# The input norm of an encoder layer, split between rows and the transposed side, with the residual rows made later

## The chip, the cores and the metric

The kernel runs on one core of one Trainium2 chip. The core has five engines that work side by side, each with its own in-order stream: PE (matrix products; its weight loads are shown apart as PEld), DVE (vector), ACT (scalar functions and copies), POOL (a general engine) and SP (which issues most transfers). They wait for one another through semaphores. What counts is the time of one execution in device microseconds, as the median of several runs. Beside it stands one profiled execution with the start and length of every instruction.

## The reference

One layer of a bidirectional encoder, 512 tokens of width 1024. What matters here is its head:

```python
h = layer_norm(x, ln_in_g, ln_in_b)            # (x - mean) * rsqrt(var + eps) * g + b
mix = parallel_mixer(h, ...)                   # h @ w_in: q, k, v of two attention families, and so on
h = layer_norm(DEEPNORM_ALPHA * h + mix, ...)  # the residual uses alpha * h again
mem_n = layer_norm(mem, ...)                   # 256 memory rows, for a later attention
```

The mixer projects h into window heads (8 query heads, 2 key/value heads, with a sink) and into three groups of 8 dilated heads. Then follow memory attention and a gated convolution, which the change doesn't touch.

## The kernel before, in words

**Data.** The rows of x lie in four blocks of 128 tokens, `h[0]` to `h[3]`, two each in the tiles `oA` and `oB`, which later take the attention outputs. Every product in full precision is made of three: operands are split in a rounded half (`hi`, a cast on ACT) and the rest (`lo`, a subtraction on DVE), and hi·hi, hi·lo and lo·hi are summed. So h is wanted transposed (feature on the partition) in two tiles, `Thi` and `Tlo`, and each weight as `hi` and `lo`.

**The prologue** (up to the line 505) makes h, its transposed halves, and the value projection of dilated group 0 on the way: 4 blocks times 24 products of 512 columns, called `hh` (hi weight, hi h), `lh` (hi weight, lo h) and `hl` (lo weight, hi h), into `g` tiles for blocks 0 and 1 and one `s` tile for blocks 2 and 3. For each block there are the statistics (`stats`, DVE; for block 3 `sums`, on ACT), the reciprocal deviation on POOL (`power`, L109), `gain` (L341, L343: subtract the mean, times g, two halves of 512) and `shift` (L348: times the deviation, plus b) on DVE, `turn` (eight 128x128 transposes on PE, L355, into the PSUM tiles `t` and `o`), `t_hi` (cast on ACT, L362) and `t_lo` (DVE, L367). g and b are spread over all partitions by products with a matrix of ones (L387, L390). `spill` (L371) writes alpha·h to memory through ACT, a block at a time, and with it the residual for later. `v_hi` and `v_lo` (L282) split the value weights. Before the first product PE is given small filler products (`busy`), as many as `WARM` says. PE, DVE and ACT all follow the written order here; the block is under a manual schedule.

**The mixer** follows from line 936 on. PE's order is still as written: projections of 24 products are cut into by *items*, pieces of attention work that wait in a queue until their inputs have been ready for some products. The item A0 is the first of the near dilated group: scores on PE, a row minimum on DVE (L725), exponentials on ACT (L728), transposes of the result on PE (L682). W0 is the first window item (L815, L819, the same lines for transposes). Each projection of a q or k ends in a rotation (`rope`): a product with the cosines on DVE (L528), a shuffle on DVE (L529), a product (L530) and a sum (L531) on POOL. DVE, ACT, POOL and SP are not ordered by hand here: a list scheduler places their instructions by its own cost estimates, and what it chose is then their fixed order. Weight loads go through SP into a ring of three buffers (`raw`). The 512 KB tiles for gains and shifts share two buffers under the tag `gb`.

Of the kernel before, what the change touches and what calls it, by code (L numbers as in the profile page):

```python
# [72 lines left out]
def hymba_layer(ctx: ExitStack, tc: tile.TileContext, A, cst_d, out):  # L73
# [173 lines left out]
    nc.gpsimd.memset(ones_t, 1.0)
# [6 lines left out]
    gin = wpool.tile([P, D], F32, tag="gb", bufs=2, name="gin")  # L254
    gt = halves(gin)
    sbt = s_tile()
    bt = [sbt[:, n, :] for n in range(2)]
# [78 lines left out]

    def gain(b):
        th = halves(h[b])
        for i in range(2):
            if ("mu", b) in LN:  # L340
                nc.vector.scalar_tensor_tensor(th[i], th[i], LN["mu", b], gt[i], ALU.subtract, ALU.mult)  # L341
            else:
                nc.vector.scalar_tensor_tensor(th[i], th[i], LN["nm", b], gt[i], ALU.add, ALU.mult)  # L343

    def shift(b):
        th = halves(h[b])
        for i in range(2):
            nc.vector.scalar_tensor_tensor(th[i], th[i], LN["rs", b], bt[i], ALU.mult, ALU.add)  # L348
# [15 lines left out]
    def t_lo(b):
        for i, src in enumerate(LN["T", b]):
            hi, lo = (t[:, 4 * i : 4 * i + 4, b * P : (b + 1) * P] for t in hT)
            nc.vector.tensor_tensor(lo, src, hi.bitcast(F32), ALU.subtract)  # L367
# [1192 lines left out]
```

## Time and profile before

| | us |
|---|---|
| median of 3 runs (lowest, highest) | 910.73 (910.62, 910.97) |
| the profiled execution | 911.27 |
| its span | 909.5 |
| PE busy in the span | 896.6 |
| DVE busy | 560.2 |
| ACT busy | 385.0 |
| first product of the value projection starts at | 13.10 |
| first product of the mixer starts at | 40.16 |

The span runs from the first to the last instruction on the engines; the execution's own time is somewhat longer. A row of a time line gives the start, the length, the engine, the line and operation, the output and the inputs with their sizes, the count of such instructions in a row and, in brackets, how long the engine was idle just before and what ended that. A row of groups gives, after the bar, the sum of busy time in us and the mean of one in ns, then the idle time before them. Names are those of the program's tiles: `Thi`, `Tlo` are the halves of h transposed, `raw`, `hi`, `lo` a weight and its halves, `zs` a tile of scratch, `mx` the memory rows.

### The profile page before, as it was taken

What the parts mean: (1) busy time and instruction counts of PE and PEld (TensorE: products, weight loads), DVE (VectorE), ACT (ScalarE), POOL (GpSimd) and SP (SyncE); (2) the same over time, 40 slices, a digit from 0 to 9 for tenths busy, and PEclk for the clock granted to TensorE, in tenths of its full rate; (3) what the DMA queues carried; (4) which work ended last, traced back from release to release, by engine and by line L of the source; (5) the groups of instructions that cost most, each with busy time, mean ns of one, the idle gap of its engine ahead of it and who ended that gap; (6) DMA issues with size and microseconds to landing.
All of it is one profiled execution on the core that took longest, in us unless ns stands there. A gap on an engine that the chain in (4) does not pass through costs nothing.

```text
span 909.5 us, 12905 instructions
## 1 busy us (share of the span) xinstructions
PE 896.6 (99%) x5097; PEld 768.3 (84%) x5097; DVE 560.2 (62%) x956; ACT 385.0 (42%) x672; POOL 127.2 (14%) x106
## 2 busy tenths in 40 slices
PE   9999999999999999999999999999999999999996
PEld 7778987898878798788988889799999999888885
DVE  7975146335446667869466576877777767433346
ACT  4563436415545576315454224344444345222210
POOL 1064033431443420010000010000000000000001
PEclk9999999999999999999999999999999999999999
DMA  6762041214221337316222304233333354223201
GB/s 220 225 213 70 24 139 47 73 67 117 70 70 47 93 117 233 138 46 171 85 70 70 93 25 129 82 93 93 95 114 94 96 160 140 93 93 103 83 23 70
DMA packets 116942, 92.84 MB, mean 102 GB/s; under 512 B 12472, under 2 KB 100752, under 8 KB 116882
## 3 DMA queue, kind: packets, MB, share of 16 engines
q1 hardware_dynamic: 116048, 89.80, 32.4%
q10 hardware_dynamic: 834, 2.22, 0.6%
q8 instruction: 40, 0.66, 0.3%
q14 instruction: 20, 0.16, 0.1%
HBM read 87.82 MB, written 4.19 MB: 101 GB/s over the span
## 4 chain that ended last, share of the span: by engine, by line
PE 95%; DVE 3%; ACT 1%; DMA 1%; issue 0%; POOL 0%; DVEq 0%; ACTq 0%
PE g L168 54%; PE s L168 24%; PE o L168 5%; PE t L168 4%; PE o L694 3%; PE s L682 2%; PE s L208 1%; DMA vt<-in_ln_in_g_dram 1%; PE s L1225 0%; DVE lo L282 0%; DVE oA L348 0%; DVE st L312 0%; DVE Tlo L367 0%; POOL zs L530 0%; DVE mx L1206 0%
## 5 line engine op out<-in xcount | busy, mean ns | idle before, releaser
L138 DVE TENSOR_TENSOR lo<-raw,hi 128x1024 fp32r<-128x1024 f32 x126 | 157.2, 1249 | 86.6 <-ACT hi L136 85.9
L136 ACT CAST hi<-raw 128x1024 fp32r<-128x1024 f32 x126 | 132.3, 1051 | 141.5 <-PE g L168 92.5
L168 PE MATMUL g<-Thi,hi 128*128 128x512 f32 x240 | 94.8, 395 | 0.0
L168 PE MATMUL g<-Tlo,hi 128*128 128x512 f32 x240 | 94.2, 393 | 0.0
L168 PE MATMUL g<-Thi,lo 128*128 128x512 f32 x240 | 94.0, 392 | 0.0
L109 POOL TENSOR_TENSOR rs<-ve,mhalf 128x1 f32<-128x1 f32 x18 | 15.3, 852 | 524.9 <-DVE ve L115 513.6
L530 POOL TENSOR_TENSOR zs<-zs,rsn 128x512 f32<-128x512 f32 x29 | 59.2, 2040 | 147.5 <-DVE zs L529 147.5
L168 PE MATMUL g<-Uhi,hi 128*128 128x512 f32 (+1 forms) x224 | 77.5, 346 | 1.0 <-ACT hi L136 1.0
L168 PE MATMUL g<-Ulo,hi 128*128 128x512 f32 (+1 forms) x224 | 77.1, 344 | 0.0
L168 PE MATMUL g<-Uhi,lo 128*128 128x512 f32 (+1 forms) x224 | 77.0, 344 | 0.0
L168 PE MATMUL g<-hi,Thi 128*128 128x512 f32 x184 | 71.6, 399 | 0.0
L168 PE MATMUL g<-hi,Tlo 128*128 128x512 f32 x184 | 70.9, 395 | 0.5 <-DVE Tlo L1173 0.5
L168 PE MATMUL g<-lo,Thi 128*128 128x512 f32 x184 | 70.7, 395 | 0.4 <-DVE lo L282 0.4
L528 DVE TENSOR_TENSOR zs<-g,rc 128x512 f32<-128x512 f32 x29 | 20.0, 689 | 68.2 <-PE g L168 31.6
L168 PE MATMUL g<-x,hi 128*128 128x256 f32 x320 | 58.8, 284 | 0.0
L168 PEld LDWEIGHTS g<-Thi,hi 128*128 128x128 f32 x240 | 45.1, 188 | 11.1 <-issue 0.9
L168 PEld LDWEIGHTS g<-Tlo,hi 128*128 128x128 f32 x240 | 45.1, 188 | 10.3 <-issue 1.4
L168 PEld LDWEIGHTS g<-Thi,lo 128*128 128x128 f32 x240 | 45.1, 188 | 9.3
L168 PEld LDWEIGHTS g<-x,hi 128*128 128x128 f32 x320 | 50.0, 192 | 0.5 <-issue 0.3
L168 PEld LDWEIGHTS g<-hi,Tlo 128*128 128x128 f32 x184 | 42.2, 230 | 6.4 <-DVE Tlo L1173 1.0
L168 PEld LDWEIGHTS g<-Uhi,hi 128*128 128x128 f32 x224 | 42.5, 190 | 5.8 <-ACT hi L136 1.2
L138 DVE TENSOR_TENSOR lo<-act,hi 128x512 fp32r<-128x512 f32 x22 | 14.8, 690 | 52.8 <-ACT hi L136 52.8
(363 smaller groups left out, 2091.8 us busy)
## 6 DMA issues: line engine op xcount, KB each, us to landing
raw<-in_w_in_dram SPq DMA_DIRECT2D x37, 512.0 KB, 3.8
raw<-in_w_gate_dram SPq DMA_DIRECT2D x22, 512.0 KB, 3.8
raw<-in_w_up_dram SPq DMA_DIRECT2D x22, 512.0 KB, 3.9
raw<-in_w_down_dram SPq DMA_DIRECT2D x22, 512.0 KB, 3.4
raw<-in_w_xk_dram SPq DMA_DIRECT2D x8, 512.0 KB, 3.9
raw<-in_w_xv_dram SPq DMA_DIRECT2D x8, 512.0 KB, 3.5
raw<-in_w_xq_dram SPq DMA_DIRECT2D x8, 512.0 KB, 4.6
raw<-in_w_xo_dram SPq DMA_DIRECT2D x8, 512.0 KB, 3.5
```

What stands on the lines that cost most here:

```text
L109: nc.gpsimd.tensor_tensor(out_, in_, mhalf, ALU.pow)
L136: nc.scalar.copy(hi, raw)
L138: (eng or nc.vector).tensor_tensor(lo, raw, hi.bitcast(F32), ALU.subtract)
L168: on_pe(nc.tensor.matmul(o, l, r, start=first, stop=last))
L208: on_pe(nc.tensor.transpose(ps[:, i // 4, f : f + P], t[:, i * P : (i + 1) * P], ident))
L528: nc.vector.tensor_tensor(zc, ps, rc, ALU.mult)
L530: nc.gpsimd.tensor_tensor(sh, sh, rsn, ALU.mult)
L682: nc.tensor.transpose(tp[:, k, :], s_, ident)
L694: nc.tensor.matmul(o[HJ[j], t0:t1], lhs(j), rhs(j), start=i == 0, stop=i == len(parts) - 1)
```

## The change

**The norm in two places.** `norm(b)` (L314) makes (x − mean)·deviation on the rows, one DVE instruction over 1024 columns in place of four over 512. Gain and shift are put on after the transpose, where a feature is a partition and g and b are one number each per partition: `t_gain` (L334 on ACT, L336 on DVE) reads the transposed PSUM tile in pieces of 128x128, since each piece has its own columns of g and b, four pieces for each half, and writes into `vt`. Then `t_hi` casts from there (L340) and `t_lo` subtracts from there (L344). ACT makes the pieces for the first half of blocks 0 and 1 and for all of blocks 2 and 3, DVE the second half of blocks 0 and 1. g and b arrive as 16 rows of 128 by two small transfers and are turned by one PE transpose into `gcol`, 128x16. The broadcast products, the two zeroings of `vt` and ACT's two copies of g are gone. All four blocks now take their statistics on DVE.

**The residual rows in the mixer.** `spill(b)` no longer copies on ACT. Since the rows in `oA` and `oB` lack g and b, four DVE instructions of 128x512 for each block (L349) make alpha·rows·g and then add alpha·b, in place, with two broadcast tiles loaded again through SP (`gb`, 512 KB each); then one transfer on ACT's queue (L350). Blocks 0 and 1 stand after the item A0 in the program, 2 and 3 after the window projection; where they come in DVE's order is up to the list scheduler, but the four of a block keep their order. The memory norm's tiles (`gm`) share the buffers of `gb`, so their loads wait for the last spill.

**Order.** The written order of the prologue is new, as is the number of fillers. In the lists below a row is a line of the program, the operation, the output and the inputs; x2 means two of them in a row.

DVE, prologue, from the split of the value weights and block 2 on (`st`, `mv`, `ve` belong to the statistics, `sm` and `nm` to the sums on ACT). Before:

```order
L282 TENSOR_TENSOR lo<-raw,hi 128x1024
L329 TENSOR_SCALAR nm<-sm 128x1
L282 TENSOR_TENSOR lo<-raw,hi 128x1024
L341 SCALAR_TENSOR_TENSOR oB<-oB,mv,gin 128x512 x2
L348 SCALAR_TENSOR_TENSOR oB<-oB,rs,s 128x512 x2
L282 TENSOR_TENSOR lo<-raw,hi 128x1024
L343 SCALAR_TENSOR_TENSOR oB<-oB,nm,gin 128x512 x2
L333 TENSOR_SCALAR ve<-sm 128x1
L367 TENSOR_TENSOR Tlo<-t,Thi 128x4x128
L367 TENSOR_TENSOR Tlo<-o,Thi 128x4x128
L282 TENSOR_TENSOR lo<-raw,hi 128x512 x2
```

and now, from the statistics of block 2 on:

```order
L309 BN_STATS st<-oB 128x6 x2
L113 BN_AGGR mv<-st 128x2
L115 TENSOR_SCALAR ve<-mv 128x1
L314 TENSOR_SCALAR oB<-oB,mv,rs 128x1024
L277 TENSOR_TENSOR lo<-raw,hi 128x1024
L344 TENSOR_TENSOR Tlo<-vt,Thi 128x4x128 x2
L309 BN_STATS st<-oB 128x6 x2
L113 BN_AGGR mv<-st 128x2
L115 TENSOR_SCALAR ve<-mv 128x1
L277 TENSOR_TENSOR lo<-raw,hi 128x512 x2
L314 TENSOR_SCALAR oB<-oB,mv,rs 128x1024
```

The last piece of the value weights (`lo` in two halves of 512) stood and stands behind `Tlo` of block 2; new between the two are the statistics of block 3.

PE, prologue, from the transposes of block 2 on. Before:

```order
L355 MATMUL t<-cst,oB 128x128 x4
L355 MATMUL o<-cst,oB 128x128 x4
L168 MATMUL g<-lo,Thi 128x512 x4
L168 MATMUL s<-hi,Thi 128x512 x8
L168 MATMUL s<-hi,Tlo 128x512 x8
L168 MATMUL s<-lo,Thi 128x512 x6
```

and now:

```order
L321 MATMUL t<-cst,oB 128x128 x4
L321 MATMUL o<-cst,oB 128x128 x4
L168 MATMUL g<-hi,Tlo 128x512 x8
L168 MATMUL g<-lo,Thi 128x512 x12
L321 MATMUL t<-cst,oB 128x128 x4
L321 MATMUL o<-cst,oB 128x128 x4
L168 MATMUL s<-hi,Thi 128x512 x8
```

All twelve remaining `hl` products of blocks 0 and 1 (`g<-lo,Thi`) now come before the products of block 2; the last eight of them use the last two pieces of the value weights.

DVE in the mixer, around the item A0 (the row minima, `ISA`). Before:

```order
L528 TENSOR_TENSOR zs<-g,rc 128x512
L529 STREAM_SHUFFLE zs<-g 128x512
L138 TENSOR_TENSOR lo<-raw,hi 128x1024
L528 TENSOR_TENSOR zs<-g,rc 128x512
L529 STREAM_SHUFFLE zs<-g 128x512
L138 TENSOR_TENSOR lo<-raw,hi 128x1024
L725 ISA pu,stT<-s,cst 128x128
```

and now:

```order
L349 SCALAR_TENSOR_TENSOR oA<-oA,gb 128x512
L138 TENSOR_TENSOR lo<-raw,hi 128x1024
L349 SCALAR_TENSOR_TENSOR oA<-gb,oA 128x512
L349 SCALAR_TENSOR_TENSOR oA<-oA,gb 128x512
L349 SCALAR_TENSOR_TENSOR oA<-gb,oA 128x512
L349 SCALAR_TENSOR_TENSOR oA<-oA,gb 128x512
L505 TENSOR_TENSOR zs<-g,rc 128x512
L506 STREAM_SHUFFLE zs<-g 128x512
L349 SCALAR_TENSOR_TENSOR oA<-gb,oA 128x512
L349 SCALAR_TENSOR_TENSOR oA<-oA,gb 128x512
L138 TENSOR_TENSOR lo<-raw,hi 128x1024
L702 ISA pu,stT<-s,cst 128x128
```

Seven of the eight instructions of the first two spills stand ahead of the first row minimum, the eighth between the minima. Before W0's row minima (L792 now) the eight of blocks 2 and 3 stand in the same way. The diff, with what only renames left out:

```diff
-WARM = (12, 3)
+WARM = (11, 7)
...
-    rows = vt.rearrange("p (v n) f -> p v n f", v=2)
-    for v in range(2):
-        (nc.vector, nc.gpsimd)[v].memset(rows[:, v], 0.0)
+    gcol = cpool.tile([P, 2 * KD], F32, name="gcol")
+    rows = zs[0 : 2 * KD, 1, 0:P]
...
-    def gain(b):
-        th = halves(h[b])
-        for i in range(2):
-            if ("mu", b) in LN:
-                nc.vector.scalar_tensor_tensor(th[i], th[i], LN["mu", b], gt[i], ALU.subtract, ALU.mult)
-            else:
-                nc.vector.scalar_tensor_tensor(th[i], th[i], LN["nm", b], gt[i], ALU.add, ALU.mult)
-
-    def shift(b):
-        th = halves(h[b])
-        for i in range(2):
-            nc.vector.scalar_tensor_tensor(th[i], th[i], LN["rs", b], bt[i], ALU.mult, ALU.add)
+    def norm(b):
+        nc.vector.tensor_scalar(h[b], h[b], LN["mu", b], LN["rs", b], ALU.subtract, ALU.mult)
...
+    def scaled(b):
+        return vt[:, 2 * (b % 2) : 2 * (b % 2) + 2, :].rearrange("p a (k t) -> p (a k) t", k=4)
+
+    def t_gain(b, i, eng):
+
+        for k in range(4 * i, 4 * i + 4):
+            g, o, src = gcol[:, k : k + 1], gcol[:, KD + k : KD + k + 1], LN["T", b][i][:, k % 4, :]
+            if eng is nc.scalar:
+                nc.scalar.activation(scaled(b)[:, k, :], src, AF.Identity, scale=g, bias=o)
+            else:
+                nc.vector.tensor_scalar(scaled(b)[:, k, :], src, g, o, ALU.mult, ALU.add)
+
+    def t_hi(b, i):
+        k = slice(4 * i, 4 * i + 4)
+        nc.scalar.copy(hT[0][:, k, b * P : (b + 1) * P], scaled(b)[:, k, :])
+
+    def t_lo(b, i):
+        hi, lo = (t[:, 4 * i : 4 * i + 4, b * P : (b + 1) * P] for t in hT)
+        nc.vector.tensor_tensor(lo, scaled(b)[:, 4 * i : 4 * i + 4, :], hi.bitcast(F32), ALU.subtract)
 
     def spill(b):
-        ah = oW[:, 2 * (b % 2) : 2 * (b % 2) + 2, :].rearrange("p a f -> p (a f)")
-        nc.scalar.activation(ah, h[b], AF.Copy, scale=ALPHA)
-        nc.scalar.dma_start(h_dram[b * P : (b + 1) * P, :], ah)
+        for i, th in enumerate(halves(h[b])):
+            for a, c, op in ((th, gb[0][i], ALU.mult), (gb[1][i], th, ALU.add)):
+                tc.keep_in_program_order(nc.vector.scalar_tensor_tensor(th, a, ALPHA, c, ALU.mult, op))
+        nc.scalar.dma_start(h_dram[b * P : (b + 1) * P, :], h[b])
...
-            nc.scalar.dma_start(rows[0:1, v].rearrange("p n f -> p (n f)"), A[name].partition_broadcast(1))
+            nc.scalar.dma_start(rows[v * KD : (v + 1) * KD, :], A[name].rearrange("(k p) -> k p", p=P))
...
-        gps = [g_tile(), g_tile()]
-        for n in range(2):
-            mm(gps[n], ones_t, rows[:, 0, n, :], True, True)
-            nc.scalar.copy(gt[n], gps[n])
-        for n in range(2):
-            mm(bt[n], ones_t, rows[:, 1, n, :], True, True)
+        gps = g_tile()[:, 0 : 2 * KD]
+        nc.tensor.transpose(gps, rows, ident[0 : 2 * KD, 0 : 2 * KD])
...
+        norm(2)
         w_raw("k", KB)
-        hh(1, *all_k)
+        w_raw("q", QB)
+        turn(2)
+        t_gain(2, 0, nc.scalar)
+        t_gain(2, 1, nc.scalar)
+        v_lo(2)
         lh(1, *all_k)
...
+        t_hi(2, 0)
+        t_hi(2, 1)
+        t_lo(2, 0)
+        t_lo(2, 1)
+        hl(1, 0, 1, 2, 3)
+        stats(3)
+        v_lo(3)
+        norm(3)
         for b in range(2):
-            hl(b, 0, 1, 2, 3)
...
+            hl(b, 4, 5, 6, 7)
...
-        spill(3)
+    gb = gb_tiles(A["ln_in_g"], A["ln_in_b"])
...
         add("A0", keys_a(0), item_a(0))
+        spill(0)
+        spill(1)
         proj(("ka",), w_cols(w_in, KA), NAT, ka)
         proj_va()
         add("W0", [("w", 0), ("ka",)], item_w(0))
         proj_w(0)
+        spill(2)
+        spill(3)
```

More of the change, by code (lines that the diff above doesn't have):

```diff
@@ L245, in hymba_layer @@
     zs = mkv.tile([P, 4, S], F32, tag="km", name="zs")
-    ones_t = zs[:, 0, 0:P]
+    ones_t = zs[:, 3, 0:P]
     nc.gpsimd.memset(ones_t, 1.0)
     vt = mkv.tile([P, NB, 512], F32, tag="vm", name="vt")
-    rows = vt.rearrange("p (v n) f -> p v n f", v=2)
-    for v in range(2):
-        (nc.vector, nc.gpsimd)[v].memset(rows[:, v], 0.0)
     for t, value in ((mhalf, -0.5), (ones, 1.0), (halfpi, HALF_PI)):
         nc.gpsimd.memset(t, value)
[L254 to L257, printed above, removed]
+    gcol = cpool.tile([P, 2 * KD], F32, name="gcol")
+    rows = zs[0 : 2 * KD, 1, 0:P]
     wv0 = []
@@ L431, in hymba_layer @@
         stats(0)
-        gain(0)
-        shift(0)
         v_hi(0)
+        nc.vector.tensor_copy(gcol, gps)
+        norm(0)
         turn(0)
-        t_hi(0)
+        t_gain(0, 0, nc.scalar)
         stats(1)
-        t_lo(0)
+        t_hi(0, 0)
+        t_gain(0, 1, nc.vector)
+        t_lo(0, 0)
         v_hi(1)
-        busy(3, vps[1])
+        t_hi(0, 1)
+        norm(1)
+        t_lo(0, 1)
+        busy(4, vps[1])
         hh(0, 0, 1)
@@ L446, in hymba_layer @@
         lh(0, 2, 3)
+        turn(1)
         v_hi(3)
-        gain(1)
-        shift(1)
+        v_lo(0)
         hh(0, 4, 5)
         lh(0, 4, 5)
+        t_gain(1, 1, nc.vector)
+        t_gain(1, 0, nc.scalar)
         hh(0, 6, 7)
-        turn(1)
-        t_hi(1)
         lh(0, 6, 7)
+        t_hi(1, 0)
+        t_hi(1, 1)
+        v_lo(1)
+        t_lo(1, 0)
+        t_lo(1, 1)
+        hl(0, 0, 1, 2, 3)
         stats(2)
-        sums(3, 0)
-        t_lo(1)
-        v_lo(0)
+        hh(1, *all_k)
+        norm(2)
         w_raw("k", KB)
-        hh(1, *all_k)
-        lh(1, *all_k)
-        neg_mean(3)
-        sums(3, 1)
-        v_lo(1)
-        w_raw("q", QB)
-        for b in range(2):
-            hl(b, 0, 1, 2, 3)
-        gain(2)
-        shift(2)
-        spill(0)
-        turn(2)
-        t_hi(2)
-        v_lo(2)
-        for b in range(2):
-            hl(b, 4, 5)
+        w_raw("q", QB)
[3 more added lines that the diff above has]
+        v_lo(2)
+        lh(1, *all_k)
+        t_hi(2, 0)
[6 more added lines that the diff above has]
+        norm(3)
+        for b in range(2):
+            hl(b, 4, 5, 6, 7)
+        for b in range(2):
+            nc.scalar.copy(vt[:, b, :], vps[b])
+        w_hi("k")
+        turn(3)
+        t_gain(3, 0, nc.scalar)
+        t_gain(3, 1, nc.scalar)
         hh(2, *all_k)
-        gain(3)
-        root(3)
-        t_lo(2)
         lh(2, *all_k)
-        w_hi("k")
-        v_lo(3)
-        spill(1)
-        shift(3)
-        hl(2, 0, 1, 2, 3, 4, 5)
-        turn(3)
-        t_hi(3)
+        t_hi(3, 0)
+        t_hi(3, 1)
         w_lo("k")
-        t_lo(3)
-        nc.vector.tensor_scalar_mul(nsnk, snk, -1.0)
-        for b in range(3):
-            hl(b, 6, 7)
+        t_lo(3, 0)
+        t_lo(3, 1)
+        hl(2, *all_k)
         w_hi("q")
         w_lo("q")
-        for b in range(2):
-            nc.scalar.copy(vt[:, b, :], vps[b])
+        nc.vector.tensor_scalar_mul(nsnk, snk, -1.0)
         hh(3, *all_k)
@@ L500, in hymba_layer @@
         hl(3, *all_k)
-        spill(2)
         rc, rsn = rope
-        posi = zs[:, 0, :].bitcast(I32)
-        nc.sync.dma_start(posi, A["positions"].partition_broadcast(P)[:, 0, :])
         ang = zs[:, 2, :]
```

30 lines of the change are left out of this document (4 added, 26 removed).

## The prediction

> **What bounds the kernel now.** I read the page's shares first, then its chain of waits.
>
> ```profile
> PE 896.6 (99%) x5097; PEld 768.3 (84%) x5097; DVE 560.2 (62%) x956; ACT 385.0 (42%) x672; POOL 127.2 (14%) x106
> PE 95%; DVE 3%; ACT 1%; DMA 1%; issue 0%; POOL 0%; DVEq 0%; ACTq 0%
> ```
>
> PE is busy for 99% of the span. The change removes four broadcast products from PE and hardly anything else there, so it can only change how long PE waits. Where does it wait? A stretch of the prologue tells (PE, PEld, DVE, ACT, POOL busy, clock, DMA share, GB/s):
>
> ```profile
> 25.00:30.00 5.00, 4.51 (x23) 3.43 (x22) 5.00 (x9) 3.08 (x4) 0.54 (x1) 1.00 0.92 300
> ```
>
> DVE is full (5.00 of 5.00) just where PE has a hole. The chain in order of time says the same: it starts in a transfer, and up to 26.4 us it runs almost wholly through DVE, then stays on PE.
>
> ```profile
> 1.96 4.69 DMA vt<-in_ln_in_g_dram
> 25.22 1.15 DVE lo L282
> 26.41 1.19 PE g L168 x4
> ```
>
> So the question is when DVE and ACT hand PE its operands, in the prologue and in the first part of the mixer, where the change puts the residual rows.
>
> **The change, part by part.** PE's rows give the frame:
>
> ```profile
> 13.10 0.71 PE L168 MATMUL g<-hi,Thi 128*128 128x512 f32 x2
> 17.11 0.60 PE L355 MATMUL t<-cst,oA 128*128 128x128 f32 x4
> 17.57 0.63 PE L355 MATMUL o<-cst,oA 128*128 128x128 f32 x4
> 36.53 1.98 PE L168 MATMUL s<-hi,Tlo 128*128 128x512 f32 x8
> 38.35 1.98 PE L168 MATMUL s<-lo,Thi 128*128 128x512 f32 x8
> 40.16 0.39 PE L168 MATMUL g<-Thi,hi 128*128 128x512 f32 x1
> ```
>
> Eight products step by 38.35 − 36.53 = 1.82 us, 0.2275 each; four transposes by 0.46, 0.115 each. From the first product (13.10) to the mixer's first (40.16) are 27.06 us. The 96 products need 21.84, the 24 transposes of blocks 1 to 3 need 2.76, two or three short fillers about 0.3: 24.9, so before waits 2.15 there.
>
> Prices of DVE, ACT and POOL:
>
> ```profile
> 8.54 1.61 DVE L341 SCALAR_TENSOR_TENSOR oA<-oA,mv,gin 128x512 f32<-128x512 f32 x2 [2.40 <-ACT gin L388]
> 11.88 1.28 DVE L312 BATCH_NORM_STATS2 st<-oA 128x6 f32<-128x512 f32 x2
> 14.11 0.68 DVE L367 TENSOR_TENSOR Tlo<-o,Thi 128x512 fp32r<-128x512 f32 x1
> 16.03 1.40 DVE L348 SCALAR_TENSOR_TENSOR oA<-oA,rs,s 128x512 f32<-128x512 f32 x2
> 21.36 1.22 DVE L282 TENSOR_TENSOR lo<-raw,hi 128x1024 fp32r<-128x1024 f32 x1
> 37.27 0.43 DVE L510 TENSOR_SCALAR zs<-zs 128x512 f32<-128x512 f32 x1
> 13.67 0.55 POOL L109 TENSOR_TENSOR rs<-ve,mhalf 128x1 f32<-128x1 f32 x1 [6.84 <-DVE ve L115]
> ```
>
> ```profile
> L1352 ACT ACTIVATE c<-g,cwT 128x512 f32<-128x512 f32 x13 | 10.0, 772 | 0.0
> L658 ACT COPY vg<-g 128x512 f32<-128x512 f32 x8 | 4.7, 588 | 23.7 <-PE g L168 23.7
> L1071 ACT COPY kmT<-g 128x256 f32<-128x256 f32 x8 | 2.9, 368 | 0.0
> L1217 DVE TENSOR_SCALAR px<-px,dn 128x256 f32<-128x256 f32 x16 | 4.9, 348 | 0.1
> ```
>
> A 128x128 piece of the gain on ACT is not in this trace. From 512 to 256 columns a copy falls by 0.22, so 128 columns are 0.26; scale and bias as columns add 0.772 − 0.588 = 0.18: 0.44 alone, about 0.36 back to back if neighbours overlap by some 0.08. Below, a quarter of the 512 row is 0.15; above, 0.44. I take 0.36, since the three rows lie on one line. The DVE piece lies between 0.17 (half of 0.348) and 0.348; two columns and a source in PSUM put it at the upper end, 0.34. The 128x1024 row norm takes 0.75 to 0.8 (twice 0.43, less one fixed part; the two-operand 1.22 is its upper bound). Stats with their small followers are about 1.75 (two halves 1.28, then 0.4 of small operations).
>
> *First product.* Before, gain and shift of block 0 wait for a broadcast gain (2.40 idle at 8.54). Now the gain is two small transfers behind the constants, landing at 7.2 to 7.5 by the 4.69 us of the old one. Then: PE transpose and DVE copy to 8.0, norm(0) to 8.9, seven fillers and turn(0) on PE to 10.2, four ACT pieces 1.4, the cast of 0.6. First product at 12.5: **−0.6**.
>
> *DVE behind it.* In order, from 8.1: norm(0) 8.9, stats(1) 10.6, four pieces 12.0, Tlo (behind the cast) 13.1, norm(1) 13.9, Tlo 14.6, v_lo(0) 15.8, four pieces 17.2, v_lo(1) 18.4, two Tlo 19.6, stats(2) 21.4, POOL's root 0.55, norm(2) done 22.9. PE reaches turn(2) after 28 products (6.37), 8 transposes (0.92), fillers (0.3) and about 0.5 of waiting for v_lo, at 20.7: it waits 2.1. After turn(2) (23.8) ACT alone does eight pieces, 23.6 to 26.5, and the first cast to 27.1. DVE has nothing ahead of Tlo(2) in its order but v_lo(2), done at 23.9, and stands idle until 27.1; then two Tlo, stats(3) to 30.1 and only then v_lo(3), whose halves are ready at 30.8 and 31.4. PE needs them after 14 products, at 27.0: it waits 3.8, and 0.8 more at the second half. Sum of waits 0.5 + 2.1 + 3.8 + 0.8 = 7.2 against 2.15, so 5.1 more, less 0.6: the mixer starts **4.5** later, at 44.7. With pieces at 0.15 the ACT run is 1.7 shorter: +2.8. With 0.44 it is 0.6 longer: +5.1; a norm of 1.22 adds 0.4. The four spill copies that leave ACT give PE nothing: nothing of the chain waits for them.
>
> *Spill beside A0's softmax.* Seven 128x512 operations with two operands stand on DVE ahead of A0's first score reduction, an eighth between the reductions. Before:
>
> ```profile
> 51.98 0.68 DVE L528 TENSOR_TENSOR zs<-g,rc 128x512 f32<-128x512 f32 x1
> 53.22 1.20 DVE L138 TENSOR_TENSOR lo<-raw,hi 128x1024 fp32r<-128x1024 f32 x1
> 56.74 0.69 DVE L528 TENSOR_TENSOR zs<-g,rc 128x512 f32<-128x512 f32 x1 [2.31 <-issue]
> 59.10 0.29 DVE L725 CUSTOM_DVE_ANT_0 pu<-s,cst 128x128 f32<-128x128 f32 x1
> ```
>
> ```profile
> 61.70 0.49 ACT L728 ACTIVATE pu<-pu,stT 128x256 f32<-128x256 f32 x1
> 63.09 1.69 PE L682 MATMUL s<-cst,pu 128*128 128x128 f32 x14
> ```
>
> DVE's hole here is only 2.31. Counted from the mixer's start (40.16): last q rope done 13.1, reductions from 18.9, the sixth exponential (61.70 + 0.49) done 22.0, PE asks at 22.9: slack 0.9. Now 13.2 + one spill operation (0.66) + lo 1.14 + four (2.64) = 17.6, ka rope 18.9, two more 20.2, lo 21.35: reductions 2.4 late, 3.1 with the eighth, less 0.9: PE waits 2.2. That is the lower bound (1.5 if the eighth hides). But DVE and POOL do not run freely beside each other here:
>
> ```profile
> 53.41 2.17 POOL L530 TENSOR_TENSOR zs<-zs,rsn 128x512 f32<-128x512 f32 x1 [0.20 <-DVE zs L529]
> 55.65 1.28 POOL L531 TENSOR_TENSOR x<-zs 128x512 f32<-128x512 f32 x1
> 189.12 1.70 POOL L530 TENSOR_TENSOR zs<-zs,rsn 128x512 f32<-128x512 f32 x1 [1.01 <-DVE zs L529]
> 189.58 2.32 DVE L138 TENSOR_TENSOR lo<-raw,hi 128x1024 fp32r<-128x1024 f32 x1
> ```
>
> POOL's rope product takes 1.28 beside an idle DVE, 2.17 beside a two-operand lo; lo takes 2.32 beside a POOL product, against 1.22. One waits for the other. [...]
>
> If they alternate: spill 13.9, POOL 15.0, lo 16.1, POOL 17.2, four spills 19.8, ka rope 21.1, spill 21.8, POOL 22.9, spill 23.5, POOL 24.6, lo 25.7: 6.8 late, 7.5 with the eighth, sixth exponential at 29.5, while PE (whose scores come 0.4 later) asks at 23.4: it waits 6.1, 6.5 with the scores. I take **+5**, near the upper end because the rows show the exclusion; bounds 1.5 and 6.5.
>
> *Spill beside W0.* The same eight operations again.
>
> ```profile
> 79.38 0.69 DVE L528 TENSOR_TENSOR zs<-g,rc 128x512 f32<-128x512 f32 x1 [2.99 <-PE g L168]
> 86.12 0.60 ACT L819 ACTIVATE pu<-pu,ast 128x385 f32<-128x385 f32 x1
> 89.59 1.58 PE L682 MATMUL s<-cst,pu 128*128 128x128 f32 x13
> ```
>
> Slack: 89.59 − 86.72 = 2.9. Eight operations 5.3, less the hole of 2.99: 2.3 late, hidden. With four POOL products of 1.1 in between 6.7 late: a wait of 3.8. PE's own wait at A0 gives DVE time to catch up: **+2**, bounds 0 and 3.8.
>
> *Other parts.* The memory norm moves behind W0's softmax. Its gain transfers now wait on SP's queue for the last spill, about 90 to 95 us, with weight loads behind them.
>
> ```profile
> L904 PE MATMUL s<-cst,oB x8: 270/272/273, 284.6 to 285.3; 128*128 128x128 f32 x8
> 114.68 1.05 ACT L136 CAST hi<-raw 128x1024 fp32r<-128x1024 f32 x1 [0.82 <-PE g L168]
> ```
>
> PE wants the memory rows at 284.6, and the next group's weights are cast from 114.68: some 20 us cover it. The two 512 KB loads of gain and shift are queued before the mixer's weights and cost nothing as long as those arrive three buffers ahead; uncovered, some 2 us.
>
> *Sum:* 4.5 + 5 + 2 = 11.5. The profiled execution's 911.27 becomes 922.8; the median shown lies 0.54 below it, so **922**.
>
> **Rivals.**
> 1. *DVE and POOL hardly exclude each other with the new operations.* Then +4.5, +2.2, 0: 917.4. For it: the lo at 53.22 keeps its 1.20 beside POOL, so DVE need not be the one that loses. Against it: the 2.32.
> 2. *Faster: DVE is the bound, and what is saved on it comes off the end.* Saved: 16 gain and shift operations (16 × 0.70 = 11.2), the zeroing of 0.92; added: four norms 3.1, eight pieces 2.7, stats(3) 1.75. That is 4.5 less DVE work before the mixer, and if PE follows DVE's total, with the spills in holes, 906. For it: DVE is full from 25 to 30 us. Against it: in the new order DVE is not full, it waits for ACT from 24 to 27, and v_lo(3) is queued behind that wait. It decides if ACT's eight pieces and two casts end before 24.5.
> 3. *The sizes are small on both sides:* pieces at 0.15, the reductions' lateness taken up by slack: −0.6 + 1.5 or so, 911 to 912.
> 4. *PE's clock falls in the 3.8 us wait.*
>
> ```profile
> 0.99 4.97 PE L168 MATMUL t<-zs 128*128 128x128 f32 x24 [0.99 <-POOL zs L247]
> 10.30 0.83 PE L168 MATMUL t<-zs 128*128 128x128 f32 x6
> ```
>
> At the start 24 fillers took 0.207 each, later 0.138: PE starts slow. If the wait cools it, about 3 us of products run at half rate, +1.6: 924. [...]
>
> **How the numbers follow.** Main case (three terms, 919 to 926) 0.52; rival 1 (914 to 919) 0.26; rival 2 0.09; rival 3 0.05, within 0.2%; rival 4 0.08. Two runs of this kernel can be told apart by about 0.2%, 1.8 us. Faster 0.09, same 0.05, slower 0.86. The main case's own range, from its bounds, is 911.27 + 2.8 + 4 + 1 − 0.5 = 918.5 up to 926; to hold 8 in 10 it must reach into rival 1: 914 to 926.
>
> **What would show it.** In the changed kernel's profile: the first product near 12.5; PE's wait before turn(2) put down to the norm and one of about 4 us put down to v_lo's lo near 27 to 31; DVE idle from about 24 to 27 behind ACT's pieces; the mixer's first product near 44.7. Near 65 us DVE full with spill operations, POOL's rope products at about 2 us, and PE waiting for A0's exponentials by 2 to 6. Wrong would be: ACT pieces under 0.25, spill operations that stay at 0.7 beside a POOL that stays at 1.3, or a PE that is busy through 60 to 95 us.

## The result

The changed kernel takes 926.45 us (median of five, 925.41 to 927.25) beside 910.85 for the kernel before: a ratio of 1.017, with a 95% interval of 1.0155 to 1.0184. It is slower, as forecast, and by more: 15.6 us where 11.5 were forecast. The time lies 0.45 us above the upper end of the range.

The profile page of the changed kernel has 5 us more of PE work and 10 us more of PE waiting:

```profile
PE 901.8 (97%) x5098; PEld 772.2 (83%) x5098; DVE 576.2 (62%) x970; ACT 386.8 (42%) x686; POOL 124.6 (13%) x105
```

PE has one instruction more than before, yet it is busy 5.2 us longer. That is the first thing to explain. The time line of PE shows where the waits are (start, length, what ran, idle before and what ended it):

```profile
11.11 0.73 PE L168 MATMUL g<-hi,Thi 128*128 128x512 f32 x2 [0.92 <-ACT Thi L340]
21.44 0.66 PE L321 MATMUL t<-cst,oB 128*128 128x128 f32 x4 [1.73 <-DVE oB L314]
29.15 3.10 PE L168 MATMUL g<-lo,Thi 128*128 128x512 f32 x6 [3.42 <-DVE lo L277]
44.18 0.39 PE L168 MATMUL g<-Thi,hi 128*128 128x512 f32 x1
60.61 1.95 PE L168 MATMUL s<-x 64*64 64x128 f32 x20
70.77 0.45 PE L659 MATMUL s<-cst,pu 128*128 128x128 f32 x1 [3.90 <-DVE stT L702]
71.90 3.10 PE L659 MATMUL s<-cst,pu 128*128 128x128 f32 x13 [0.69 <-ACT pu L705]
90.65 1.78 PE L168 MATMUL s<-ka,x 64*128 64x256 f32 x12
102.97 2.56 PE L659 MATMUL s<-cst,pu 128*128 128x128 f32 x13 [0.76 <-ACT pu L796]
113.07 1.95 PE L168 MATMUL s<-x 64*64 64x128 f32 x20
```

The first row is the first product. Then come the wait for the norm of block 2 and the wait for the last value weights. 44.18 is the mixer's first product, 40.16 before. Then A0's scores, its transposes behind 3.90 and 0.69 of waiting, W0's scores, W0's transposes, and the next item's scores. In the kernel before, the scores of A0, of W0 and of the next item are these rows:

```profile
56.99 1.95 PE L168 MATMUL s<-x 64*64 64x128 f32 x20 [0.34 <-POOL x L531]
79.27 1.78 PE L168 MATMUL s<-ka,x 64*128 64x256 f32 x12
98.04 1.95 PE L168 MATMUL s<-x 64*64 64x128 f32 x20
```

The steps between these points:

| stretch | before | changed | more |
|---|---|---|---|
| start to the mixer's first product | 40.16 | 44.18 | 4.02 |
| from there to A0's scores | 16.83 | 16.43 | −0.40 |
| A0's scores to W0's | 22.28 | 30.04 | 7.76 |
| W0's scores to the next item's | 18.77 | 22.42 | 3.65 |
| the rest of the execution | 813.23 | 813.74 | 0.51 |

The last row is the profiled execution's time less the point before it (911.27 and 926.81). All but half a microsecond is lost before 113 us, in the three places that the prediction named.

The row at 71.90 holds what it did not forecast. Thirteen transposes take 3.10 us there; the fourteen of the kernel before took 1.69. The granted clock explains it. Stretches of the changed kernel, cut within 0.15 us of where the clock changes (PE, PEld, DVE, ACT, POOL busy, clock, DMA share, GB/s):

```profile
25.90:29.30 3.40, 0.15 (x1) 0.15 (x1) 3.33 (x8) 0.17 (x1) 0.65 (x1) 1.00 0.00 0
67.00:70.40 3.40, 0.00 (x0) 0.00 (x0) 3.40 (x9) 1.01 (x5) 0.69 (x1) 0.98 0.06 17
70.40:73.80 3.40, 2.35 (x10) 1.88 (x11) 1.46 (x10) 2.96 (x13) 0.35 (x2) 0.50 0.84 292
73.80:77.10 3.30, 3.30 (x12) 2.82 (x11) 0.00 (x0) 1.89 (x4) 0.41 (x3) 0.50 0.00 0
100.90:104.30 3.40, 2.12 (x12) 1.15 (x11) 3.40 (x13) 3.21 (x13) 0.00 (x0) 1.00 1.04 275
104.30:107.70 3.40, 3.40 (x16) 3.33 (x16) 2.08 (x3) 3.40 (x7) 3.07 (x2) 0.51 0.38 148
```

After 3.4 us almost without work the clock is 0.50 for one or two stretches of 3.4 us, and it is 0.50 once more behind W0's waits. Together with one such stretch from 29.3 to 32.7 there are four, and half of 4 × 3.4 is 6.8 us of PE time at most. Part of it falls on time in which PE waits anyway. In the last microseconds the clock is 0.50 as well, in the kernel before from 906.4 on, in the changed kernel from 920.2 on; that is left out in what follows.

### The profile page after: what moved, and what is told of

Read it like the earlier page. It is cut to its first block, busy times and chain, and to the rows that moved or that the text cites. A ratio compares the mean times of both kernels' runs of the same rounds, so it can differ in the third digit from the quotient of the medians.

```text
span 925.0 us, 12927 instructions
## 1 busy us (share of the span) xinstructions
PE 901.8 (97%) x5098; PEld 772.2 (83%) x5098; DVE 576.2 (62%) x970; ACT 386.8 (42%) x686; POOL 124.6 (13%) x105
## 4 chain that ended last, share of the span: by engine, by line
PE 85%; DVE 1%; ACT 1%; issue 0%; DVEq 0%; ACTq 0%
PE g L168 48%; PE s L168 22%; PE o L168 5%; PE t L168 4%; PE o L671 2%; PE s L659 2%; PE s L208 1%; PE s L1206 0%; ACT pu L705 0%; ACT pu L751 0%; DVE mx L1187 0%; PE s L881 0%; ACT hi L136 0%; PE t L659 0%; PE o L822 0%
## 5 line engine op out<-in xcount | busy, mean ns | idle before, releaser
L138 DVE TENSOR_TENSOR lo<-raw,hi 128x1024 fp32r<-128x1024 f32 x126 | 163.3, 1298 | 93.8 <-ACT hi L136 93.3
L168 PE MATMUL g<-Ulo,hi 128*128 128x512 f32 (+1 forms) x224 | 77.1, 344 | 0.0
L507 POOL TENSOR_TENSOR zs<-zs,rsn 128x512 f32<-128x512 f32 x29 | 56.2, 1938 | 154.7 <-DVE zs L506 147.9
L168 PEld LDWEIGHTS g<-lo,Thi 128*128 128x128 f32 x184 | 43.0, 235 | 9.6 <-DVE lo L277 5.0
L168 PEld LDWEIGHTS g<-hi,Thi 128*128 128x128 f32 x184 | 42.3, 231 | 6.3 <-ACT Thi L340 1.1
```

Source lines behind the costliest of these rows:

```text
L138: (eng or nc.vector).tensor_tensor(lo, raw, hi.bitcast(F32), ALU.subtract)
L168: on_pe(nc.tensor.matmul(o, l, r, start=first, stop=last))
L507: nc.gpsimd.tensor_tensor(sh, sh, rsn, ALU.mult)
```

## Experiments

Their ratios to the kernel before are compared with the 1.017 of the changed kernel, since the kernel before itself took 910.9 to 911.6 us on the chips used.

### The order on DVE in the prologue

```diff
         v_lo(2)
+        stats(3)
+        v_lo(3)
         lh(1, *all_k)
...
         hl(1, 0, 1, 2, 3)
-        stats(3)
-        v_lo(3)
         norm(3)
```

> Edit: on DVE the statistics of block 3 and the split of the last value weights go ahead of Tlo of block 2, into the 3.06 us in which DVE waited for ACT; nothing else moves. Theory (PE's long wait of the prologue comes from the order on DVE: v_lo(3) stood behind Tlo(2) and stats(3)): the 3.42 us wait before the lo products goes, turn(3) waits about 0.8 us for its norm instead, and without a wait of 3.4 us the clock stays full: the mixer's first product at 39.6 instead of 44.2, the time 4.6 lower, near 922. Rival (ACT's eight pieces and two casts set the pace and the order on DVE only decides whose name stands at the wait): a wait of 3 us or more remains before turn(3), the mixer starts at 43 or later, the time is at most 1.5 lower.

Measured: 921.49 beside 911.61, ratio 1.0109 (1.0094 to 1.0124), 5.6 us better than the changed kernel. Its PE time line:

```profile
27.75 0.63 PE L321 MATMUL t<-cst,oB 128*128 128x128 f32 x4 [0.64 <-ACT vt L462]
39.58 0.39 PE L168 MATMUL g<-Thi,hi 128*128 128x512 f32 x1
56.62 1.95 PE L168 MATMUL s<-x 64*64 64x128 f32 x20 [0.56 <-POOL x L508]
66.77 0.30 PE L659 MATMUL s<-cst,pu 128*128 128x128 f32 x1 [3.90 <-DVE stT L702]
```

The 3.42 us wait is gone, 0.64 stands before the transposes of block 3, and the mixer starts at 39.58, as the theory said (39.6). So ACT's eight pieces did not make the long wait: the DVE work queued behind them, `stats(3)` and `v_lo(3)`, did. A0's wait is the same 3.90, so it doesn't depend on the prologue. The gain is 1.0 more than forecast, and not for the forecast's reason. Of the 4.60 that the mixer starts earlier, 3.99 reach A0's scores, where PE now waits 0.56 for POOL. The rest comes from the clock in the mixer: with the prologue's slow stretch two more are gone, since the clock is at 0.50 for one stretch behind A0 (67.5 to 70.9; thirteen transposes take 3.10 at 67.91) instead of two, and for none behind W0 (thirteen transposes take 2.08 at 97.94; 2.56 in the changed kernel). The steps from A0's scores to W0's and from there to the next item's are 1.04 and 1.12 shorter (29.00 and 21.30).

### The clock in the prologue's wait

Two runs put filler products before the last `lo` products; the second has half as many, since a filler is two instructions in the trace:

```diff
-        for b in range(2):
-            hl(b, 4, 5, 6, 7)
+        hl(0, 4, 5)
+        busy(12, vps[3])
+        hl(0, 6, 7)
+        hl(1, 4, 5, 6, 7)
```

> Edit: 24 small filler products on PE in the long wait of the prologue, into a tile that is overwritten later; the wait itself stays as long. Theory (the clock's fall is a cost of its own: the granted clock was 0.5 from 29.3 to 32.7): the fillers keep the clock at 1.00 there, the lo products end some 1.6 us earlier, the mixer starts at 42.5 instead of 44.2, the time is 1.7 lower, near 924.8. Rival (the low clock is only how an idle PE is reported, or does not follow from idleness): the clock falls all the same, the time within 0.5 of 926.45.

With 24 fillers: 925.51 beside 911.61, ratio 1.0153 (1.0138 to 1.0168), an interval that overlaps that of the changed kernel. The fillers ran past the wait and the mixer started at 44.13, so this run says little of the prologue.

> Edit: as before with half as many filler products, 12, since a filler showed as two instructions in the trace and 24 of them ran past the wait of 3.4 us. Theory (the clock's fall is a cost of its own): no half clock near 30 us, turn(3) starts 1.6 us earlier than in the changed kernel (30.4 instead of 32.05). What that makes of the whole time depends on how many windows at half clock follow in the mixer, one window of 3.41 us costing 1.7. Rival: turn(3) stays at 32.

With 12 fillers: 924.75 beside 911.03, ratio 1.0149 (1.0135 to 1.0163), 1.9 us better than the changed kernel, though the two intervals overlap.

```profile
29.37 2.03 PE L168 MATMUL g<-lo,Thi 128*128 128x512 f32 x6 [0.73 <-DVE lo L277]
31.24 0.60 PE L321 MATMUL t<-cst,oB 128*128 128x128 f32 x4
43.04 0.39 PE L168 MATMUL g<-Thi,hi 128*128 128x512 f32 x1
60.58 2.04 PE L168 MATMUL s<-x 64*64 64x128 f32 x20 [0.94 <-POOL x L510]
```

Six products take 2.03 instead of 3.10 from nearly the same start, and the clock stays full. The transposes of block 3 start at 31.24 instead of 32.05 (30.4 expected), and the mixer 1.14 earlier. But A0's scores start at 60.58, where they started without the fillers (60.61): they wait 0.94 for the rotation on POOL. What the prologue gains here is waited away in the mixer; the gain of the whole comes from later, where only one stretch at half clock followed (71.4 to 74.8; thirteen transposes take 3.10 at 71.87): the steps at A0 and at W0 are 1.02 and 1.13 shorter (29.02 and 21.29). About 1.1 of that is lost again in the profiled execution, in a wait of 1.02 for the next item's softmax.

### The clock at A0

```diff
         yield 18
+        if c == 0:
+            fill = ps_tile("t", 1)
+            for _ in range(14):
+                mm(fill[:, 0:P], ident, ident, True, True)
```

> Edit: 30 small filler products on PE ahead of A0's transposes, into a free tile; the spill and the wait for the softmax stay. Theory (of A0's 7.8 us some 4.6 are the wait and 3.2 the two windows at half clock): the clock stays full from 70 to 77 us, 3 us lower, near 923.4; if the transposes do not count as work for the clock, it falls once less at least, 1.6 or more lower. Rival (the clock does not matter beside the wait): within 0.7 of 926.45.

With 30 fillers, sized before the doubling was known: 925.5 beside 911.61, ratio 1.0153 (1.0136 to 1.017), which overlaps the changed kernel's interval. They ran until 74.55. By the run that follows, the softmax is ready 11.3 us behind A0's scores (72.14 − 60.86), here at 61.76 + 11.3 = 73.0, so they ran 1.5 us too long. W0's scores still came 29.08 behind A0's (90.84 − 61.76), not later than the 30.04 of the changed kernel: the clock stayed full there (twelve transposes take 1.47 at 74.77), and the useless work took the place of time lost to it. In the prologue of this execution the clock was at 0.50 for two stretches, 28.3 to 35.2 (eight products take 2.80 at 33.63, 1.98 at full clock), and the mixer started at 45.33, so the whole says little.

> Edit: 14 filler products, about the length of the wait, on PE ahead of A0's transposes; spill and wait stay. Theory: the clock stays full from 70 to 77 us, W0's scores start 3 us earlier against A0's scores than in the changed kernel (27.0 us behind them instead of 30.0; 22.3 in the kernel before). Rival (the transposes are slow for want of their inputs, not of clock): they stay 30 behind.

With 14: 923.5 beside 911.03, ratio 1.0138 (1.0124 to 1.0152), 2.9 us better.

```profile
66.94 3.29 PE L168 MATMUL t<-cst 128*128 128x128 f32 x28
71.01 0.30 PE L659 MATMUL s<-cst,pu 128*128 128x128 f32 x1 [0.78 <-DVE stT L702]
72.14 2.02 PE L659 MATMUL s<-cst,pu 128*128 128x128 f32 x13 [0.83 <-ACT pu L705]
88.79 1.78 PE L168 MATMUL s<-ka,x 64*128 64x256 f32 x12
110.08 1.95 PE L168 MATMUL s<-x 64*64 64x128 f32 x20
```

and the stretch behind the wait:

```profile
70.40:73.80 3.40, 1.90 (x13) 1.36 (x14) 1.71 (x12) 3.19 (x13) 0.38 (x2) 1.00 0.87 295
```

The transposes start when they did, behind the same softmax, but the clock is 1.00 and they take 2.02 instead of 3.10. W0's scores come 27.93 behind A0's (88.79 − 60.86) instead of 30.04; 27.0 were expected. So of A0's 7.76 us, 2.1 are the clock and 5.65 the wait and what comes with it. Between none and two slow stretches stand two runs with one: 29.00 (new order on DVE) and 29.02 (12 fillers), so a stretch costs about 1.05 here. The clock does not fall behind W0 either (thirteen transposes take 2.08 at 101.11; 2.56 in the changed kernel), and that step is 21.29 instead of 22.42, so 1.13 of its 3.65 are the clock.

### No arithmetic in the spill

The sixteen instructions are left out, so that the residual lacks alpha, gain and shift:

```diff
         for i, th in enumerate(halves(h[b])):
-            for a, c, op in ((th, gb[0][i], ALU.mult), (gb[1][i], th, ALU.add)):
-                tc.keep_in_program_order(nc.vector.scalar_tensor_tensor(th, a, ALPHA, c, ALU.mult, op))
```

> Edit: the sixteen DVE instructions of the spill are left out, only its transfers stay, so that the residual lacks alpha, gain and shift and the output is not the reference's. Theory (the spill beside POOL delays the softmax of A0 and of W0, and the two waits cool the clock): both waits go and the clock stays full after 40 us, 7.8 us at A0 and 3.7 us at W0 come back, the prologue's 4.0 stay: 915.0. Rival (the late prologue itself, or the rotation on POOL, delays the softmax): A0's wait shrinks by less than half, 920 or more.

Measured: 918.59 beside 911.61, ratio 1.0076 (1.0061 to 1.0091). From A0's scores to W0's are 22.28 us and from there to the next item's 18.77, both as before the change: the whole loss in the mixer belongs to these instructions. The total misses 915.0 by 3.6 for another reason. With nothing to wait for, the list scheduler put block 0's transfer into ACT's stream ahead of the pieces:

```profile
10.20 0.36 ACTq L347 DMA_DIRECT2D h_dram<-oA  x1
10.61 1.51 ACT L334 ACTIVATE vt<-t,gcol 128x128 f32<-128x128 f32 x4 [3.58 <-DMA raw<-in_w_in_dram]
```

In the changed kernel the pieces start at 8.90. The first product here is at 12.82 instead of 11.11, behind a wait of 2.25, and the clock falls for one stretch behind this wait (13.9 to 17.3; two products take 1.05 at 14.63, 0.62 at 18.16) as well as for one behind the wait of 3.42 (34.4 to 37.8; eight products take 2.66 at 36.56, 1.98 at 42.71); the mixer starts at 48.15. Leaving work out moved other work; only the stretches behind it can be compared.

### POOL taken out of the spill's way

```diff
+        eng = nc.vector if rn[0] in (2, 3, 4, 5) else nc.gpsimd
-        nc.gpsimd.tensor_tensor(sh, sh, rsn, ALU.mult)
-        nc.gpsimd.tensor_tensor(view[1](dest), view[0](zc), view[0](sh), ALU.add)
+        eng.tensor_tensor(sh, sh, rsn, ALU.mult)
+        eng.tensor_tensor(view[1](dest), view[0](zc), view[0](sh), ALU.add)
```

> Edit: in the changed kernel the product and the sum of four rotations (second to fifth, those beside the spills) are made by DVE instead of POOL, so DVE has 4 more instructions beside each spill and POOL none. Theory (DVE and POOL shut each other out: four of DVE's instructions there lost 1.08 us each): without POOL the first row minimum of A0 starts at 65.0 instead of 68.7 although DVE has more to do, A0's transposes start near 68 instead of 70.8, the time 3 to 5 lower. Rival (the spill operations themselves fill DVE, POOL beside it costs little): four times 0.6 more on DVE, the row minimum at 69.5 or later, the time 0.8 or more higher.

Measured: 920.74 beside 911.4, ratio 1.0102 (1.0088 to 1.0116): 6.2 us better (3 to 5 expected), although DVE does eight instructions more. First DVE in the changed kernel, then DVE and PE's wait in this one:

```profile
57.10 2.31 DVE L138 TENSOR_TENSOR lo<-raw,hi 128x1024 fp32r<-128x1024 f32 x1
59.34 1.77 DVE L349 SCALAR_TENSOR_TENSOR oA<-gb,oA 128x512 f32<-128x512 f32 x1
64.78 1.78 DVE L349 SCALAR_TENSOR_TENSOR oA<-oA,gb 128x512 f32<-128x512 f32 x1
66.49 2.29 DVE L138 TENSOR_TENSOR lo<-raw,hi 128x1024 fp32r<-128x1024 f32 x1
68.70 0.28 DVE L702 CUSTOM_DVE_ANT_0 pu<-s,cst 128x128 f32<-128x128 f32 x1
```

```profile
62.98 0.69 DVE L349 SCALAR_TENSOR_TENSOR oA<-oA,gb 128x512 f32<-128x512 f32 x1
63.58 1.22 DVE L138 TENSOR_TENSOR lo<-raw,hi 128x1024 fp32r<-128x1024 f32 x1
65.32 0.28 DVE L703 CUSTOM_DVE_ANT_0 pu<-s,cst 128x128 f32<-128x128 f32 x1
```

```profile
68.65 2.02 PE L660 MATMUL s<-cst,pu 128*128 128x128 f32 x13 [1.43 <-ACT pu L706]
```

Beside POOL, two spill operations take 1.77 instead of 0.69 and two subtractions 2.3 instead of 1.22; without it all that stand beside the spill have their own length. The first row minimum starts at 65.32 (65.0 expected, 68.70 in the changed kernel, 69.5 by the rival). PE's wait shrinks to 1.43, and the clock does not fall there. From A0's scores to W0's are 24.33 us (60.86 to 85.19), so of the 5.65 at full clock 3.6 go with POOL out of the way: the exclusion was the larger half of A0's loss. The clock doesn't fall behind W0 either (four transposes `o<-cst,x` take 0.66 at 99.11; 1.06 at 106.18 in the changed kernel); by the run with 14 fillers that and the full clock at A0 are worth 1.1 and 2.1 of the gain.

### The spill elsewhere, and versions that beat the kernel before

The computation is whole in the next four. First the spill alone: block 0's arithmetic into DVE's idle time of the prologue, blocks 1 to 3 behind the second value group, the memory loads later, and the loads of `gb` ahead of the prologue.

```diff
         w_lo("k")
+        spill_math(0)
         t_lo(3, 0)
...
-        spill(0)
-        spill(1)
...
-        spill(2)
-        spill(3)
...
         v_group(1)
-        mem_load(0)
+        for b in range(1, 4):
+            spill(b)
...
         proj_b("q", 0, 3)
+        mem_load(0)
```

> Edit: the computation is whole; the spill of block 0 goes into DVE's idle time of the prologue, those of blocks 1 to 3 behind the second value group, where DVE is idle from 120 to 130 us, the memory loads behind them. The prologue's order is that of the changed kernel. Theory (the spill costs what it does only by its place beside POOL and ahead of the softmax): no wait at A0 and W0, the prologue's 4.0 stay: 4.0 above the kernel before, about 915. Rival (16 more instructions cost DVE time wherever they are, since it feeds PE): 918 or more.

Measured: 915.88 beside 911.03, ratio 1.0053 (1.0039 to 1.0066).

```profile
45.64 0.39 PE L168 MATMUL g<-Thi,hi 128*128 128x512 f32 x1
62.19 1.95 PE L168 MATMUL s<-x 64*64 64x128 f32 x20
68.28 1.69 PE L664 MATMUL s<-cst,pu 128*128 128x128 f32 x14
84.47 1.78 PE L168 MATMUL s<-ka,x 64*128 64x256 f32 x12
```

A0's transposes take 1.69 with no wait, and W0's scores come 22.28 behind A0's, as before the change. The same instructions cost nothing in their new places: the profiled execution is 5.2 above that of the kernel before, and A0's scores are 5.2 later. What is left is the prologue: in this execution the slow clock lasted two stretches there (28.9 to 35.7; its mean is 0.50 from 29.3 to 32.7 and 0.56 from 32.7 to 36.1), so the mixer starts at 45.64.

Then both mends together, with the statistics of block 2 ahead of `Tlo` of block 1:

```diff
         v_lo(1)
-        t_lo(1, 0)
-        t_lo(1, 1)
         hl(0, 0, 1, 2, 3)
         stats(2)
+        t_lo(1, 0)
+        t_lo(1, 1)
```

> Edit: the spills as in the run with late spills, the prologue as in the run with the new order on DVE, and the statistics of block 2 ahead of Tlo of block 1. Theory (both losses are losses of order, and the norm in two places itself gains): the mixer starts at 39.1 (40.16 before), no wait at A0 and W0, about 1.0 below the kernel before. Rival (the gain of the earlier first product is used up by the pieces on ACT and by the spill elsewhere): within 0.5 of the kernel before, or above it.

Measured: 909.91 beside 911.03, ratio 0.9985 (0.9976 to 0.9994).

```profile
38.81 0.39 PE L168 MATMUL g<-Thi,hi 128*128 128x512 f32 x1
55.43 1.95 PE L168 MATMUL s<-x 64*64 64x128 f32 x20
77.72 1.78 PE L168 MATMUL s<-ka,x 64*128 64x256 f32 x12
```

The mixer starts at 38.81 (39.1 expected), W0's scores stand at 77.72 (79.27 before), and the clock doesn't fall (its mean is 0.999). So with its order and its spill mended, the kernel with the norm in two places is about 1.1 us faster than the kernel before. No run gave the kernel before a new order of its own, so how much of this only the norm in two places can give is not shown.

Third, the prologue's last two waits: statistics and norm of block 2 earlier, covered by the hi products of block 1; block 3's transposes behind the hi products of block 2, and `v_lo(3)` ahead of `stats(3)`.

```diff
+        stats(2)
         v_lo(1)
-        hl(0, 0, 1, 2, 3)
-        stats(2)
-        t_lo(1, 0)
-        t_lo(1, 1)
+        hl(0, 0, 1)
         hh(1, *all_k)
+        hl(0, 2, 3)
         norm(2)
+        t_lo(1, 0)
+        t_lo(1, 1)
...
+        hh(2, *all_k)
         turn(3)
         t_gain(3, 0, nc.scalar)
         t_gain(3, 1, nc.scalar)
-        hh(2, *all_k)
```

> Edit: the version with both mends, and further in the prologue: statistics and norm of block 2 ahead of the second split of value weights, block 1's hi products moved up to cover them, the transposes of block 3 behind block 2's hi products. Theory (PE's waits before the two transposes, 1.00 and 0.64, are order too): they go, the mixer starts near 37, 1.5 to 2 lower than the version with both mends, near 908 beside 911. Rival (the rotations and their angles on DVE and POOL are what A0's scores then wait for): a wait of 0.5 to 1 us put down to POOL before A0's scores, the gain under 1.0.

Measured: 909.7 beside 911.4, ratio 0.998 (0.9971 to 0.9989), not told apart from the version before it. The mixer starts at 37.31, 1.5 us earlier, but the rival holds:

```profile
47.77 0.69 DVE L511 TENSOR_TENSOR zs<-g,rc 128x512 f32<-128x512 f32 x1 [0.85 <-ACT rc L501]
49.27 0.47 PE L168 MATMUL g<-Thi,hi 128*128 128x512 f32 x1 [0.92 <-DVE zs L512]
55.46 1.95 PE L168 MATMUL s<-x 64*64 64x128 f32 x20 [0.47 <-POOL x L514]
```

DVE's first rotation waits for the cosines (`rc`), PE for the tile that the rotation reads, and A0's scores for POOL. They start at 55.46, where they started in the version before it (55.43): all of the prologue's gain is waited away again.

Last, the angles of the rotations are begun where the spill of block 0 stood, and that spill follows them:

```diff
         w_lo("k")
-        spill_math(0)
+        rc, rsn = rope
+        ang = zs[:, 2, :]
+        nc.vector.tensor_copy(ang, posi)
...
         t_lo(3, 0)
```

> Edit: the last version further: the angles of the rotations are begun in DVE's idle time of the prologue, where the spill of block 0 stood, and that spill follows them. Theory (since the mixer starts at 37.3, what binds is the cosine and sine tile, ready only at 47.7): the two waits of 0.92 and 0.47 in the mixer's first part go, 1.0 to 1.4 lower than the last version, 2.7 to 3.1 below the kernel before. Rival (the weight casts on ACT, which wait for transfers, hold the sines up anyway): as the last version, within 0.4.

Measured: 908.82 beside 911.3, ratio 0.9974 (0.9964 to 0.9984), 2.5 us below the kernel before (2.7 to 3.1 expected). The wait of 0.92 is gone; the other remains:

```profile
54.54 1.95 PE L168 MATMUL s<-x 64*64 64x128 f32 x20 [0.53 <-POOL x L513]
```

A0's scores start 0.9 earlier than in the version before it. This is the lowest time of any version run, though its interval overlaps those of the two versions before it.

## Why the prediction was right in direction and too low

**First product: wrong size, in the other direction.** Forecast 12.5, measured 11.11: 2.0 earlier than before instead of 0.6. The step had the two rows of gain and shift land at 7.2 to 7.5. In the changed kernel they are issued at 1.18 and 1.79, right behind the constants at 0.73, and PE's transpose of them starts at 6.19, so they are in place more than 1 us before what I took. The price of the pieces was right: four take 1.51 us (`vt<-t,gcol ... x4` at 10.61 above), 1.4 were forecast.

**DVE behind it: the waits right, the sum right by luck.** Waits of 0.5, 2.1 and 3.8 + 0.8 were forecast; 0.31, 1.73 and 3.42 were measured and none for the second half, with the DVE row behind them just as told:

```profile
25.58 1.29 DVE L344 TENSOR_TENSOR Tlo<-vt,Thi 128x512 fp32r<-128x512 f32 x2 [3.06 <-ACT Thi L340]
```

DVE stands idle for 3.06 us until ACT's cast, with v_lo(3) behind it. The order run shows that the queueing on DVE, not ACT's pieces, was the cause of the long wait. The mixer's start was forecast at 44.7 and is 44.18, but two errors nearly cancel there: the first product is 1.4 earlier than forecast, and about 1.1 is the slow clock, as the run with 12 fillers shows (43.04).

**Spill beside A0: right.** +5 was forecast, between 1.5 for no exclusion and 6.5 for full alternation; at full clock it is 5.65. The reductions were forecast 25.7 after the mixer's start with alternation and 21.35 without; they came 24.5 after it. The run without POOL beside the spill settles that the difference is the exclusion. One reading was off: the row of 1.28 at 55.65 is POOL's sum, not its product, but the product beside an idle DVE takes as long (1.30 at 49.49 in the kernel before).

**Spill beside W0: right.** +2 was forecast, 0 to 3.8; at full clock W0's stretch is 21.29 us in the run with 14 fillers (88.79 to 110.08), 2.5 more than before.

**What failed: the clock, which the sum put at nothing.** What counts of the prologue is how late A0's scores come, and that is 3.6 with the slow stretch (60.61 against 56.99) and 3.6 without it (60.58 with 12 fillers), since PE then waits 0.94 for the rotation on POOL. So at full clock the three terms are 3.6, 5.65 and 2.5, together 11.8 beside the forecast 11.5. The half clock adds 2.1 behind A0 and 1.1 behind W0, together 3.2; with the 0.5 behind 113 us this makes the measured 15.5 of the profiled executions. The prediction did name the clock as its fourth rival, but gave it 0.08, one place and one stretch (+1.6), in the prologue, where it turned out to cost nothing at A0's scores. The 3 us at half rate behind that 1.6 were my estimate: the kernel before shows 0.50 only in its last 3.1 us (906.4 to 909.5), behind the end of PE's work. The changed kernel showed 0.50 from 29.3 to 32.7, worth 1.14 at the mixer's first product (44.18 against 43.04 with 12 fillers). Its own main case held two waits of about 4 and 5 us. A wait of that length and the half clock behind it are one event, and they should have been one term. The range shows the same gap: its upper end of 926 is the sum of the three upper bounds (5.1, 6.5 and 3.8) with nothing for the clock. The kernel before has no such wait, and the three last versions, which have none either, keep the clock full (means of 0.999, 0.998 and 0.998; 0.998 in the kernel before).

The stretches lie on a grid. In the changed kernel the clock is at 0.50 from 29.3 to 32.7, from 70.3 to 77.1 and from 104.4 to 107.8, each one or two times 3.41 us, and 29.3, 70.3 and 104.4 lie 12 and 10 such lengths apart (75.1 us for the 22). Idleness alone does not account for the falls. The stretches of 3.41 us ahead of the first two hold 0.15 and 0.01 us of PE work, but the one ahead of the third holds 2.1, nearly all transposes, and in the run without the spill's arithmetic the clock also falls behind stretches with 1.2 and 1.4 us of products. Had the sum held one stretch for each of the waits of 3.8 and about 5, at the 1.6 of the fourth rival each, it would have come to about 925 (an estimate: 922 + 2 × 1.6).

**The rivals.** The first, little exclusion and 917.4, falls with the rows of 1.77 and 2.3. The second, DVE's saved work coming off the end, falls too: DVE was not full but waiting at 22.5 to 25.6. The mended versions are faster than the kernel before (down to 0.9974), but they change the order as well, so that the saved work is what they gain is not shown. The third, small sizes on both sides, falls with the A0 wait.

## What to carry to other kernels

Work that is taken off an in-order engine can be worth nothing until the order is remade: here much the same instructions cost 15 us in one order and gain 2.5 in another. Before new instructions are put into an idle engine's time, look at what stands right behind them in its queue, and at what POOL does just then if the engine is DVE: the split of a weight (`lo<-raw,hi`, 128x1024) took 2.31 us beside it and 1.22 without it. Price every longer wait of PE that you forecast together with the half clock that can follow: here each wait of 2.25 us or more was followed by it, and waits of up to 2.12 were not (2.25 and 2.12 both in the run without the spill's arithmetic), save for the two short ones among W0's transposes.

## What the runs showed of the hardware that was not expected

**The clock fell behind one stretch of transposes and stayed full behind another.** The clock changes on a grid of 3.41 us (29.3, 70.3 and 104.4 in the changed kernel, 12 and 10 lengths apart; 13.9 and 34.4 in the run without the spill's arithmetic, 6 apart), so each execution can be cut into stretches of that length. W0's softmax gives PE the same two waits of about 0.5 and 0.8 us in the changed kernel and in the runs with fillers and with the new order on DVE. In the changed kernel the grid falls so that the stretch with these waits (101.0 to 104.4) holds 2.1 us of PE work, nearly all transposes, and the clock falls behind it. In the other five runs the stretch with these waits holds as much work, 2.2 us, but 1.0 to 1.3 of it are products, and the clock stays full (W0's last thirteen transposes take 2.08 in each of the five, 2.56 in the changed kernel). Yet behind A0's wait in the run with 14 fillers, the stretch from 70.69 to 74.10 holds 2.2 us of work, all but 0.2 of it transposes, and the clock stays full (1.00 from 70.4 to 73.8). Why it fell behind the one and not behind the other, no run here shows.

**The number of such stretches differs between executions.** The profiled execution of the changed kernel has four, at a mean clock of 0.990. One stretch is 0.0018 of that mean (half of 3.41 in 925 us), so the two executions at 0.992 and 0.993 (925.69 and 925.41) have one or two fewer than the three at 0.990 (926.45 to 927.25); that is an estimate, since only one of the five has a trace. The prologue's wait of 3.4 us gave one stretch in four profiled executions and two in two. In the four it ended before the slow stretch began (at 29.15 and 29.30 in the changed kernel), in the two it reached 0.42 and 0.83 us into it (late spill, 30 fillers).

**Useless PE work can cost less than the idle time it fills.** The 30 fillers at A0 ran 1.5 us beyond the wait, and W0's scores came 29.08 behind A0's: 1.15 later than with 14 fillers, but 0.96 earlier than with none, where the clock fell.
